# Two of the four weight sums of layer 0's feed-forward units made by accumulating DMAs

## The chip, the cores and the metric

One core of a Trainium2 chip runs the whole program. The metric is the device time of one execution in microseconds, the median over the runs. The engines of a core are TensorE (PE in the profile, with PEld for its weight loads), VectorE (DVE), ScalarE (ACT), GpSimd (POOL) and SyncE (SP). Here SP issues nearly all loads of weights, and POOL issues a few DMAs and small copies.

## The reference

Two layers of a diffusion transformer, in float32, over 512 tokens of x and 256 tokens of context, with a width of 1024 and a hidden width of 2816:

```python
def swiglu(h, w_up, w_down):
    a, b = jnp.split(h @ w_up, 2, axis=-1)
    return (jax.nn.silu(a) * b) @ w_down

def layer(x, ctx, mod_x, mod_c, cos, sin, g1, g2, w_in, ...):
    hx = rmsnorm(x, g1) * (1 + sc1) + sh1
    ...
```

Each layer has a normalisation that is modulated by six vectors (from the matrix w_mod), three groups of heads, an output projection, and then swiglu on the normalised tokens with a residual. In layer 0 swiglu runs on all 768 tokens, in layer 1 on the 512 of x. The change concerns `h @ w_up` in layer 0.

## The kernel before, in words

Float32 products are made of three matmuls each: a tile is split into a rounded part hi (a cast on ACT, line 177) and the rest lo (a subtraction on DVE, line 188), and hi*hi, hi*lo and lo*hi are summed on PE (line 139).

The hidden width of 2816 is cut into 22 columns of 128, f = 0 to 21. For f from 2 on, a *unit* uf makes both halves of its column, the gate and the up half, with seven products where eight quarters would be multiplied plainly. The weights of a unit are two tiles of 128 x 1024, a (the gate half, quarters a11 and a12) and b (the up half, quarters a21 and a22), the quarters being halves of the width of 1024. Four of the seven products need sums of quarters: s1 = a21 + a22 in a tile of its own, e; then a21 + a11 in place, which is s3; s2 = s3 + a22, written over a11; s4 = s2 + a12, over a12. The products run in the order p1 (on a11), p5 (s1), p4 of the unit before (its a22), p6 (s2), p2 (a12), p3 (s4), p7 (s3); the parts are made in the order a11, s1, s2, a12, s4, s3, a22. Each part is cast, its rest is subtracted, and 12 matmuls use it: 128 x 384 each in layer 0, 128 x 256 in layer 1.

The weights come by SP into a ring of four raw slots of 512 KB (line 522), in the order of a plan. A slot is used again when its last reader has been issued. In layer 0 the modulation weights of w_mod go through the same ring, one or two tiles after each unit's a and b; DVE reduces them with line 199 (t<-raw,cst,t). The units are grouped in blocks of columns, by column f in layer 0: (0, 5), (5, 10), (10, 14), (14, 18), (18, 22). Columns 0 and 1 are done plainly. After each block its part of w_down follows. To keep names short, units are numbered u1 to u20 in their order here and in what follows, so u1 to u3 are in the first block, u4 to u8 in the second, u9 to u12, u13 to u16 and u17 to u20 in the others.

An item of the plan may have `sums` set (line 487). Then `w_load`, which issues the loads of an item as soon as a slot is free, takes a tile e for s1 and issues three DMAs on POOL's queue: e <- a21 (line 535), e += a22 (line 536), and in the raw tile, a21 += a11 (line 537). All three read the weights in HBM again, 256 KB each. The part s1 is then cast from e, and the additions of s1 and of a21 + a11 aren't made on DVE. Line 538 tells the planner that such an item is there 4 us later than its loads. In the kernel before only layer 1 does so.

The program is written out unit by unit, and a scheduler places the instructions of each engine, up to a certain point by hand, behind it by the instructions' dependencies and order in the text. Each engine then runs its own row of instructions in order, and stops at one that must wait.

Of the kernel before, what the change touches and what calls it, by code (L numbers as in the profile page):

```python
# [319 lines left out]
def hybrid_kernel(ctx: ExitStack, tc: tile.TileContext, x, c, cx, c_ctx, w_mod, b_mod, norm1_g, norm2_g,  # L320
# [28 lines left out]
    plan = []  # L349

    def cols(src, n):
        return lambda raw: [(raw[:, :n, :], src.rearrange("(k p) n -> p k n", p=P))]

    def w_item(key, n, load, width=P, hold=False, quarters=False):
        plan.append(dict(key=key, n=n, load=load, width=width, hold=hold, mod=False, early=False, read=False, late=False,
                         apart=False, quarters=quarters, sums=None))
# [7 lines left out]
    def mod_items(n):  # L364
        for _ in range(min(n, len(mod_todo))):
            l, g, *at_ = mod_todo.pop(0)
            if len(at_) == 2:
                half, kk = at_
                n0 = g * 512 + half * 256
                src, n_, width = w_mod[l, kk * 512:(kk + 1) * 512, n0:n0 + 256], 4, 256  # L370
            else:
                q, = at_
                src, n_, width = w_mod[l, q * 256:(q + 1) * 256, g * 512:(g + 1) * 512], 2, 512
            plan.append(dict(key=("mod", l, g, *at_), n=n_, load=cols(src, n_), width=width, hold=False, mod=True,
                             early=False, read=False, quarters=False))
# [8 lines left out]
    def in_item(l, name, col):  # L384
        if name == "lr":
            w_item((l, name), 8, lambda raw: [(raw[:, :, j * 32:(j + 1) * 32],
                                               w_in[l, :, col:col + 32].rearrange("(k p) n -> p k n", p=P))
                                              for j in range(3)], 96)
        else:
            w_item((l, name), 8, cols(w_in[l, :, col:col + P], 8))  # L390

    def q_item(l, g):
        def load(raw):
            r = []
            for kv in range(2):
                c0 = W_Q + (kv * 4 + g) * 64
                r.append((raw[:, :, kv * 64:(kv + 1) * 64],
                          w_in[l, :, c0:c0 + 64].rearrange("(k p) n -> p k n", p=P)))
            return r
        w_item((l, "q", g), 8, load)  # L400

    def out1_item(l, j):
        def load(raw):
            ms = slice(j * 256, (j + 1) * 256)
            return [(raw[:, 0:2, :], w_out[l, 0:256, ms].rearrange("(k p) n -> p k n", p=P)),
                    (raw[:, 2:4, :], w_out[l, 768:1024, ms].rearrange("(k p) n -> p k n", p=P))]
        w_item((l, "o1", j), 4, load, 256)

    def up_item(l, q):

        def load(raw):
            ks = slice(q * 2 * P, (q + 1) * 2 * P)
            return [(raw[:, :, j * 2 * P:(j + 1) * 2 * P],
                     w_up[l, ks, j * FF:j * FF + 2 * P].rearrange("(k p) n -> p k n", p=P)) for j in range(2)]
        w_item((l, "up", q), 2, load, 4 * P)
        plan[-1]["late"] = q > 0

    def out2_item(l, m, hold):
        def load(raw):
            ms = slice(m * P, (m + 1) * P)  # L420
            return [(raw[kv * 64:(kv + 1) * 64, 0:4, :],
                     w_out[l, 256 + kv * 256:512 + kv * 256, ms].rearrange("(k p) n -> p k n", p=64))
                    for kv in range(2)]
        w_item((l, "o2", m), 4, load, P, hold)
# [11 lines left out]
    def first_item(l, q):  # L436

        def load(raw):
            ks = slice(q * 2 * P, (q + 1) * 2 * P)
            r = []  # L440
            for i, name in enumerate(FIRST):
                for j in range(3 if name == "lr" else 1):
                    n, c0 = (32, IN_COL[name]) if name == "lr" else (P, IN_COL[name])
                    r.append((raw[:, :, i * P + j * n:i * P + (j + 1) * n],
                              w_in[l, ks, c0:c0 + n].rearrange("(k p) n -> p k n", p=P)))
            return r
        w_item((l, "first", q), 2, load, 3 * P + 96)
        plan[-1]["late"] = q > 0 or l == 0
        plan[-1]["apart"] = q + l == 0
# [9 lines left out]
    for l in range(DEPTH):  # L459
        for q in range(4 if l else 0):  # L460
            first_item(l, q)
        for i, name in enumerate(IN_ORDER):
            if name in FIRST:
                continue
            if name[0] == "q":
                q_item(l, int(name[1]))
            else:
                in_item(l, name, IN_COL[name])
            if l == 0 and i >= 4:
                mod_items(1)  # L470
        for j in range(4):
            out1_item(l, j)
            if l == 0:
                mod_items(2)
        for m in range(NK):
            out2_item(l, m, m >= N_OUT2)
            if l == 0 and m == 0:
                mod_items(1)
        blocks = F_BLOCKS[l]
        for bi, (f0, f1) in enumerate(blocks):  # L480
            for q in range(0 if bi else 4):
                up_item(l, q)
            for f in range(max(f0, 2), f1):
                for half, nm in ((0, "a"), (1, "b")):
                    c0 = half * FF + f * P
                    w_item((l, nm, f), 8, cols(w_up[l, :, c0:c0 + P], 8), quarters=True)
                    plan[-1]["sums"] = (l, f) if l and half else None
                if l == 0:
                    mod_items(2 if f < 14 else 1)
            for m in range(NK):  # L490
                hold = bi == len(blocks) - 1 and m >= N_DOWN
                w_item((l, "d", bi, m), f1 - f0,
                       cols(w_down[l, f0 * P:f1 * P, m * P:(m + 1) * P], f1 - f0), P, hold)
                plan[-1]["late"] = m == 1

                if l == 0 and bi < len(blocks) - 1:
                    mod_items(((0, 1, 1, 2, 1, 1, 1, 0), (0, 1, 0, 1, 0, 1, 1, 0))[bi > 1][m])
# [1570 lines left out]
```

## Time and profile before

| | |
|---|---|
| median of 3 runs | 1621.19 us (1620.47 to 1623.0) |
| profiled execution | 1616.48 us, span 1614.4 us, granted clock 0.998 |
| PE busy | 1574.5 us, 98% of the span |
| DVE, ACT, POOL busy | 1220.2, 755.2, 103.3 us |
| HBM read | 175.08 MB |
| feed-forward units of layer 0 | about 440 to 920 us of the span |
| feed-forward units of layer 1 | about 1240 to 1580 us of the span |

The profile is of one execution. A row of the groups has the line of the code, the engine, what is written and read, the count, the busy time and the mean time of one; then the idle time of the engine before these instructions and what ended most of it. A row of the timeline begins with the start and the length in us.

### The profile page before, as it was taken

Reading aid. Unit: us, or ns where it says so; the run is one execution under the profiler, and the core shown is the slowest. Engines: PE = TensorE matmul, PEld = TensorE weight load, DVE = VectorE, ACT = ScalarE, POOL = GpSimd, SP = SyncE. Lnnn points to the kernel's source line nnn. Section 1 sums busy time; section 2 is a strip of 40 time slices with the busy share of each in tenths; the row PEclk is TensorE's granted clock in tenths of the full one; section 3 lists DMA queues with packets and bytes.
Section 4 is the critical chain, followed back from the end, with each engine's and each line's share of the span. In section 5 each row is a group of like instructions: output and inputs, shape, how many; then the busy total and the mean of one; then the engine's idle time right before and its main releaser. Section 6 shows DMA issues by size and latency. Waiting matters only on the chain.

```text
span 1614.4 us, 29190 instructions
## 1 busy us (share of the span) xinstructions
PE 1574.5 (98%) x11562; PEld 1390.8 (86%) x11562; DVE 1220.2 (76%) x2426; ACT 755.2 (47%) x1588; POOL 103.3 (6%) x118
## 2 busy tenths in 40 slices
PE   7999999999999999999999999998999999999998
PEld 6878677888898899998999988786879999989898
DVE  5687877668886788688888776879787966757576
ACT  4445544453653243242433445464474744636354
POOL 2000000000000000000000000000001112213012
PEclk9999999999999999999999999999999999999999
DMA  9831312154224544435334342211124466848652
GB/s 267 253 96 26 93 53 79 55 169 124 60 79 147 154 141 138 141 123 151 95 109 130 94 123 66 54 38 42 66 76 122 89 148 150 173 121 160 150 123 92
DMA packets 277449, 184.32 MB, mean 114 GB/s; under 512 B 30788, under 2 KB 258624, under 8 KB 277312
## 3 DMA queue, kind: packets, MB, share of 16 engines
q1 hardware_dynamic: 251008, 155.93, 33.7%
q0 software_dynamic: 24480, 21.21, 7.7%
q10 hardware_dynamic: 1824, 5.31, 0.8%
q8 instruction: 91, 1.49, 0.4%
q14 instruction: 46, 0.38, 0.1%
HBM read 175.08 MB, written 7.34 MB: 113 GB/s over the span
## 4 chain that ended last, share of the span: by engine, by line
PE 72%; DVE 11%; DMA 5%; ACT 3%; issue 2%; DVEq 0%; SPq 0%; ACTq 0%
PE main L139 45%; PE bank L139 23%; DMA raw<-in_w_mod_dram 3%; DVE act L188 3%; PE bank L143 3%; DVE wlo L188 1%; DVE t L188 1%; DMA raw<-in_w_up_dram 1%; ACT t L155 1%; DVE t L199 1%; DVE t L216 1%; DVE act L199 1%; DVE mx L207 1%; ACT t L177 1%; ACT act L155 1%
## 5 line engine op out<-in xcount | busy, mean ns | idle before, releaser
L139 PE MATMUL main<-act,whi 128*128 128x512 f32 (+2 forms) x2772 | 667.3, 345 | 5.3 <-DVE act L199 2.5
L139 PEld LDWEIGHTS main<-act,whi 128*128 128x128 f32 x2772 | 460.4, 189 | 62.8 <-issue 12.0
L139 PE MATMUL main<-act,wlo 128*128 128x512 f32 (+2 forms) x1866 | 477.6, 333 | 2.3 <-DVE wlo L188 2.2
L139 PEld LDWEIGHTS main<-act,wlo 128*128 128x128 f32 x1866 | 314.8, 189 | 31.1 <-DVE wlo L188 4.2
L177 ACT CAST whi<-raw 128x512 fp32r<-128x512 f32 (+4 forms) x242 | 181.5, 751 | 292.4 <-PE main L139 200.9
L139 PE MATMUL bank<-act,whi 128*128 128x256 f32 (+4 forms) x1140 | 213.2, 309 | 1.7 <-DVE whi L188 1.0
L139 PEld LDWEIGHTS bank<-act,whi 128*128 128x128 f32 (+1 forms) x1140 | 177.5, 188 | 10.0 <-DVE whi L188 1.6
L139 PE MATMUL bank<-act,wlo 128*128 128x256 f32 (+4 forms) x930 | 182.0, 309 | 0.6 <-DVE wlo L188 0.6
L199 DVE SCALAR_TENSOR_TENSOR act<-main,mods,act 128x256 f32<-128x256 f32 (+1 forms) x162 | 99.3, 616 | 75.7 <-PE main L139 74.0
L139 PEld LDWEIGHTS bank<-act,wlo 128*128 128x128 f32 (+1 forms) x930 | 147.6, 189 | 5.5 <-DVE wlo L188 1.4
L188 DVE TENSOR_TENSOR wlo<-raw,whi 128x1024 fp32r<-128x1024 f32 (+4 forms) x122 | 122.7, 1006 | 22.3 <-ACT whi L177 21.5
L188 DVE TENSOR_TENSOR wlo<-raw,wlo 128x512 fp32r<-128x512 f32 x120 | 81.7, 687 | 39.5 <-ACT wlo L177 38.8
L199 DVE SCALAR_TENSOR_TENSOR t<-raw,cst,t 128x512 f32<-128x512 f32 x126 | 92.3, 747 | 21.3 <-DMA raw<-in_w_mod_dram 20.6
L188 DVE TENSOR_TENSOR whi<-raw,whi 128x512 fp32r<-128x512 f32 x120 | 81.4, 687 | 25.2 <-ACT whi L177 24.0
L155 ACT ACTIVATE t<-bank,nm 128x256 f32<-128x256 f32 (+1 forms) x144 | 69.8, 497 | 60.6 <-DVE nm L199 55.9
L177 ACT CAST wlo<-raw 128x512 fp32r<-128x512 f32 x120 | 74.6, 622 | 42.6 <-PE main L139 17.5
L177 ACT COPY t<-bank 128x512 f32<-128x512 f32 (+3 forms) x131 | 57.3, 452 | 71.8 <-PE bank L139 43.2
L139 PE MATMUL main<-act 128*128 128x256 f32 (+1 forms) x516 | 79.5, 308 | 0.0
L188 DVE TENSOR_TENSOR act<-t,act 128x512 fp32r<-128x512 f32 (+7 forms) x110 | 73.2, 682 | 7.0 <-ACT act L177 5.2
L155 ACT ACTIVATE t<-t 128x256 f32<-128x256 f32 (+3 forms) x108 | 58.1, 538 | 43.2 <-DVE t L188 42.5
L139 PE MATMUL main<-t,whi 128*128 128x512 f32 (+1 forms) x302 | 75.9, 338 | 0.0
L139 PEld LDWEIGHTS main<-act 128*128 128x128 f32 x516 | 70.9, 191 | 5.2 <-ACT t L155 0.4
(161 smaller groups left out, 2005.3 us busy)
## 6 DMA issues: line engine op xcount, KB each, us to landing
raw<-in_w_mod_dram SPq DMA_DIRECT2D x92, 512.0 KB, 4.2
raw<-in_w_up_dram SPq DMA_DIRECT2D x80, 512.0 KB, 4.0
raw<-in_w_in_dram SPq DMA_DIRECT2D x26, 512.0 KB, 3.9
t<-in_w_up_dram POOLq DMA_DIRECT2D x40, 256.0 KB, 5.5
raw<-in_w_down_dram SPq DMA_DIRECT2D x24, 384.0 KB, 4.0
raw<-in_w_down_dram SPq DMA_DIRECT2D x32, 256.0 KB, 2.9
raw<-in_w_down_dram SPq DMA_DIRECT2D x16, 320.0 KB, 3.4
raw<-in_w_up_dram POOLq DMA_DIRECT2D x20, 256.0 KB, 4.7
```

The lines of the kernel that those rows point to most:

```text
L139: self.pin("pe", self.nc.tensor.matmul(out, lhsT, rhs, start=start, stop=stop, **kw))
L143: self.pin("pe", self.nc.tensor.transpose(out, in_, ident))
L155: ins = self.pin("act", self.nc.scalar.activation(out, in_, func, **kw))
L177: self.pin("act", self.nc.scalar.copy(out, in_))
L188: self.pin(eng, self._v(eng).tensor_tensor(out, a, b, op))
L199: self.pin(eng, self._v(eng).scalar_tensor_tensor(out, a, s, b, op0, op1))
L207: self.pin("dve", self.nc.vector.tensor_reduce(out, in_, AX.X, op))
L216: self.pin("dve", self.nc.vector.copy_predicated(out, mask, data))
```

## The change

One condition is dropped, so that the items of layer 0 carry `sums` as well:

```diff
                     w_item((l, nm, f), 8, cols(w_up[l, :, c0:c0 + P], 8), quarters=True)
-                    plan[-1]["sums"] = (l, f) if l and half else None
+                    plan[-1]["sums"] = (l, f) if half else None
```

In the 20 units of layer 0, the 40 DVE additions that make s1 and a21 + a11 go, and 60 DMAs on POOL come in, 40 of them accumulating. Layer 1's own instructions stay as they are, as does the order of SP's loads.

On POOL, where layer 0's units had no row, the second block (u4 to u8) now stands as follows. L535 and L536 make e of a unit (t is the e tile), L537 adds into its raw b.

```order
36 L535 DMA t_6038<-in_w_up_dram 128x4x128
37 L536 DMA t_6038<-in_w_up_dram 128x4x128
38 L537 DMA raw<-in_w_up_dram 128x4x128 x2
39 L535 DMA t_6199<-in_w_up_dram 128x4x128
40 L536 DMA t_6199<-in_w_up_dram 128x4x128
41 L535 DMA t_6342<-in_w_up_dram 128x4x128
42 L537 DMA raw<-in_w_up_dram 128x4x128
43 L536 DMA t_6342<-in_w_up_dram 128x4x128
44 L535 DMA t_6483<-in_w_up_dram 128x4x128
45 L536 DMA t_6483<-in_w_up_dram 128x4x128
46 L537 DMA raw<-in_w_up_dram 128x4x128 x2
47 L535 DMA t_6630<-in_w_up_dram 128x4x128
```

The tiles t_6038, t_6199, t_6342, t_6483 and t_6630 are e of u4 to u8. Row 38 holds the L537 of u4 and of u5, row 46 that of u7 and of u8. So e of u5 (rows 39, 40) and of u8 (row 47 and the one after it) stand behind the L537 of their own unit, u6 has its L535 ahead of it and its L536 behind, and u4 and u7 have both ahead. Of the pairs x2 there are five in layer 0, at u5, u8, u10, u14 and u18; u11, u15, u16, u19 and u20 stand as u6. In layer 1 POOL's rows, which the change leaves alone, begin so:

```order
32 L537 DMA raw<-in_w_up_dram 128x4x128
33 L535 DMA t_13319<-in_w_up_dram 128x4x128
34 L535 DMA t_13460<-in_w_up_dram 128x4x128
35 L536 DMA t_13319<-in_w_up_dram 128x4x128
36 L536 DMA t_13460<-in_w_up_dram 128x4x128
37 L537 DMA raw<-in_w_up_dram 128x4x128
38 L535 DMA t_13602<-in_w_up_dram 128x4x128
39 L536 DMA t_13602<-in_w_up_dram 128x4x128
40 L537 DMA raw<-in_w_up_dram 128x4x128
```

Here the pair of a unit stands ahead of its own L537 (t_13460 is that of the unit whose L537 is row 37).

On DVE, in u8 before, with the waits in brackets: line 188's t_6663<-raw is s1, raw<-raw in row 927 is a21 + a11, and in row 929 s2; row 928 is the rest of s1.

```order
924 L188 TENSOR_TENSOR whi<-raw,whi 128x512 [waits DMAHW3_49,Activation_49]
925 L188 TENSOR_TENSOR t_6663<-raw 128x512 [waits DMAHW4_49]
926 L188 TENSOR_TENSOR t_6555<-bank,t_6555 128x384 [waits PE_49]
927 L188 TENSOR_TENSOR raw<-raw 128x512 [waits DVE_49]
928 L188 TENSOR_TENSOR wlo<-t_6663,wlo 128x512 [waits Activation_49]
929 L188 TENSOR_TENSOR raw<-raw 128x512 [waits DVE_49]
```

And in the changed kernel, where t_6630 is e:

```order
910 L188 TENSOR_TENSOR whi<-raw,whi 128x512 [waits DMAHW3_49,Activation_49]
911 L188 TENSOR_TENSOR raw<-raw 128x512 [waits DMAHW4_49,DMASW6_49,DVE_49]
912 L199 SCALAR_TENSOR_TENSOR t_6505<-raw,cst,t_6505 128x512 [waits DMAHW5_49]
913 L188 TENSOR_TENSOR t_6562<-bank,t_6562 128x384 [waits PE_49]
914 L188 TENSOR_TENSOR mods_137<-bank,bmod 128x4 [waits PE_49]
915 L199 SCALAR_TENSOR_TENSOR t_6505<-raw,cst,t_6505 128x512 [waits DVE_49]
916 L188 TENSOR_TENSOR t_6577<-main,t_6577 128x384 [waits PE_49]
917 L188 TENSOR_TENSOR wlo<-t_6630,wlo 128x512 [waits DMASW0_49,Activation_49]
```

The two additions are gone; s2's addition (row 911) now waits for a DMA of POOL (DMASW) and stands ahead of an eviction and of two steps of the modulation work; the rest of s1 (row 917) stands behind these and waits for a cast that waits for another DMA of POOL.

## The prediction

> **What bounds the kernel now.** I read the windows by stage first, then the groups of VectorE (DVE), then the POOL queue in layer 1, where the operations that the change adds already run, and last the timeline of the units that get them. The windows of the two feed-forward stages that matter (length, then busy time of PE, PEld, DVE, ACT, POOL, clock, DMA share, GB/s):
>
> ```profile
> core 0: us, PE busy (x) PEld busy (x) DVE busy (x) ACT busy (x) POOL busy (x), PEclk, DMA share, GB/s
> 440.00:920.00 480.00, 473.98 (x2812) 444.91 (x2811) 387.60 (x656) 182.78 (x332) 0.00 (x0) 1.00 0.42 124
> ...
> 1240.00:1580.00 340.00, 338.64 (x2393) 316.40 (x2392) 235.03 (x441) 175.60 (x350) 65.62 (x59) 1.00 0.64 137
> ```
>
> Layer 0's feed-forward part is bound by TensorE: of 480.00 us PE works 473.98, so 6.0 us is all that any relief of another engine can bring there. DVE is busy 387.60 us, 81%, but PE hardly ever waits for it. Layer 1 shows the scheme that layer 0 now gets, at 1.4 us of idle PE in 340, though with matmuls over a narrower tile and without the modulation weights, which in layer 0 go through the same four raw slots and DVE.
>
> **What is removed.** The two groups of DVE in that stage, of which 20 additions each go, and the wait that the modulation work has now:
>
> ```profile
> L188 DVE TENSOR_TENSOR raw<-raw 128x512 f32<-128x512 f32 x60 | 41.2, 686 | 0.7
> ...
> L188 DVE TENSOR_TENSOR t<-raw 128x512 f32<-128x512 f32 x20 | 13.8, 689 | 12.2 <-DMA raw<-in_w_up_dram 12.2
> ```
>
> ```profile
> DVE t L199 <- DMA raw<-in_w_mod_dram: 20.6, 21, 2.4
> ```
>
> 20 x 0.689 + 20 x 0.686 = 27.5 us of DVE. All of it lies beside TensorE: removing it is worth between 0 and the 6.0 us that PE idles. I take 0, because those waits stand where a late cast or an eviction comes last, not one of these sums, and keep 6.0 for the range. DVE waits 20.6 us in 21 pieces for modulation weights, so the slots are in demand: a load is issued when a reader lets a slot go.
>
> **What is added.** Per unit three DMAs of 256 KB on POOL, 60 in all, 15.7 MB over 480 us, or 33 GB/s onto 124. That is 157 GB/s, against 137 GB/s in layer 1 at a share of 0.64, so I take layer 1's durations as they are. The order on POOL decides more than the count. POOL takes its rows one by one and stops at one whose data is not there, as layer 1 shows (line, tile, and in brackets the idle time before the row and what ended it):
>
> ```profile
> 1348.23 1.29 POOL L537 DMA_DIRECT2D raw<-in_w_up_dram  x1 [7.37 <-DVE raw L188]
> 1348.98 1.32 POOL L535 DMA_DIRECT2D t<-in_w_up_dram  x1
> 1355.74 1.27 POOL L536 DMA_DIRECT2D t<-in_w_up_dram  x1 [5.44 <-DMA t<-in_w_up_dram]
> 1360.72 1.27 POOL L537 DMA_DIRECT2D raw<-in_w_up_dram  x1 [3.71 <-DMA raw<-in_w_up_dram]
> 1361.47 1.31 POOL L535 DMA_DIRECT2D t<-in_w_up_dram  x1
> 1366.83 1.27 POOL L536 DMA_DIRECT2D t<-in_w_up_dram  x1 [4.05 <-DMA t<-in_w_up_dram]
> ```
>
> ```profile
> 1355.38 0.37 SPq L522 DMA_DIRECT2D raw<-in_w_up_dram  x1
> ```
>
> ```profile
> L536 POOL DMA_DIRECT2D t<-in_w_up_dram x20: 1264/1276/1692, 1246.3 to 1557.5; - x20
> ...
> DMA to landing us min/median/max: 4.6/5.1/6.7
> ```
>
> The L537 at 1360.72 stood waiting for its raw slot, whose load SP had issued at 1355.38, 5.34 us before. L535 follows L537 by 0.75 us. L536 follows L535 by 6.76 and 5.36 us, mean 6.06, since it adds into what L535 must first have landed. Its own landing takes 5.1.
>
> A rule speaks against these prices. The Trainium skill's DMA: Bandwidth & Descriptors, in Anatomy of one DMA — SWDGE (gpsimd) path, gives a DMA of this queue as 2.0 us plus its bytes at 436 GB/s: 2.6 us for 256 KB, an estimate; by it the sum would lose some 2.5 us on each of the two, and with them the waits worked out below. The trace, with 4.6 at the least, does not agree, and the measurement decides.
>
> Now the order of the changed kernel: in layer 0 five units (u5, u8, u10, u14, u18) have L535 and L536 behind their own L537, which is to say behind the landing of their own raw b. In layer 1 the pair mostly stands ahead of it, and what stands behind an L537 is the pair of the next unit. So the sum s1, which a unit needs as its second product, p5, is made only after b has landed. The price of that chain, from the issue of b's load to the first matmul on s1, needs the load's landing in layer 0 and the cast:
>
> ```profile
> raw<-in_w_up_dram SPq DMA_DIRECT2D x80, 512.0 KB, 4.0
> ```
>
> ```profile
> 611.78 0.62 ACT L177 CAST wlo<-t 128x512 fp32r<-128x512 f32 x1 [0.75 <-DVE t L188]
> ```
>
> From b's issue to L537 lie between 4.0 us, the landing alone, and the 5.34 of layer 1; I take 4.54, the landing with half a microsecond for POOL to go on, an estimate. Then 0.75 to L535, 6.06 to L536, 5.1 to its landing, 0.62 for the cast: 17.07 us. The five issues of b and the five starts of p5 before (p5 goes into a "bank" tile, the product ahead of it into "main"; the last row of each fence is u20, used further on):
>
> ```profile
> 554.88 0.37 SPq L522 DMA_DIRECT2D raw<-in_w_up_dram  x1
> 602.72 0.37 SPq L522 DMA_DIRECT2D raw<-in_w_up_dram  x1
> 673.22 0.37 SPq L522 DMA_DIRECT2D raw<-in_w_up_dram  x1
> 769.52 0.37 SPq L522 DMA_DIRECT2D raw<-in_w_up_dram  x1
> 862.62 0.37 SPq L522 DMA_DIRECT2D raw<-in_w_up_dram  x1
> 893.23 0.37 SPq L522 DMA_DIRECT2D raw<-in_w_up_dram  x1
> ```
>
> ```profile
> 570.95 0.51 PE L139 MATMUL bank<-act,whi 128*128 128x384 f32 x2
> 615.51 1.20 PE L139 MATMUL bank<-act,wlo 128*128 128x384 f32 x6
> 689.56 0.68 PE L139 MATMUL bank<-act,wlo 128*128 128x384 f32 x3
> 784.36 0.51 PE L139 MATMUL bank<-act,wlo 128*128 128x384 f32 x2
> 876.87 0.51 PE L139 MATMUL bank<-act,wlo 128*128 128x384 f32 x2
> 905.99 0.33 PE L139 MATMUL bank<-act,wlo 128*128 128x384 f32 x1
> ```
>
> Issue plus 17.07 against p5: u5 571.95 against 570.95, 1.0 late; u8 619.79 against 615.51, 4.3; u10 690.29 against 689.56, 0.7; u14 786.59 against 784.36, 2.2; u18 879.69 against 876.87, 2.8. Together 11.0 us in which TensorE has nothing to do. This is the first term.
>
> The second term is what comes after. Six units (u6, u11, u15, u16, u19, u20) have only L536 behind their own L537: 4.54 + 0.75 + 5.1 + 0.62 = 11.0 us from b's issue. For u20 that is 904.24 against p5 at 905.99: 1.75 us in hand, and no wait by itself. But DVE and ACT take their work in order, and behind a late s1 stand the other casts, the evictions and the modulation work that frees slots. How closely a load follows that work:
>
> ```profile
> 601.16 1.53 DVE L199 SCALAR_TENSOR_TENSOR t<-raw,cst,t 128x512 f32<-128x512 f32 x2
> ...
> 612.65 0.69 DVE L188 TENSOR_TENSOR wlo<-t,wlo 128x512 fp32r<-128x512 f32 x1
> ```
>
> L199 ended at 602.69, and the b load of u8 was issued at 602.72. And s1's subtraction on DVE ended at 613.34, 2.17 us ahead of its matmul at 615.51. When s1 is late by the chain, DVE loses that lead and TensorE does not, so the next loads come up to 2.17 us later than TensorE does, each time. Between 0 (the 1.75 in hand nearly covers it) and 2.17 us for each of the six units; I take the middle, 1.1, since neither end is nearer, so 6.6 us.
>
> The third term is the other sum, a21 + a11, which L537 makes in place, and on which s2, s3 and s4 rest. Layer 1 shows what that costs for the same 20 DMAs:
>
> ```profile
>   DVE raw L188: 2.9, 6
> ```
>
> DVE waited 2.9 us for L537 in 6 of them. Layer 1 has shorter products, but also earlier loads; I take the 2.9 whole, between 0 and the double. SP's own order does not change, and the waits that its loads gain, on the slots into which POOL added, fall on sums landed long before the slot's last reader: nothing, unless POOL runs late by half a unit.
>
> The sum: 11.0 + 6.6 + 2.9 - 0 = 20.5 us on the profiled execution's 1616.48 us (span 1614.4 and 2.1 around it), 1637.0. The median of the three runs is 1621.19, 4.7 higher; with the same difference the forecast is 1621.2 + 20.5 = 1641.7 us.
>
> **The rivals.**
>
> *The sums are hidden, and the relief of DVE counts.* The place is p5 of u8, u14 and u18. If L535 and L536 take some 2.5 us less each there than in layer 1, the chain is 12 us and none of the five is late (the largest, 4.3 us, is gone), and up to 6.0 us of PE's idle time comes back: with most of it, 5, the time is 1616 us. For it speaks layer 1's 1.4 us of idle PE; against it the order, which layer 1 does not have, and the landing, 4.6 at the least. It decides from the point where the chain is under 12.8 us (615.51 - 602.72). The rule of the skill above would bring it about. Chance 0.09.
>
> *The waits and the relief cancel.* The chain is some 2.5 us shorter than I count, u8 is late by 2 and u18 by 0.3, and PE's waits shrink by as much: within 3 us of 1621. Chance 0.07.
>
> *POOL's DMAs are slower than in layer 1.* There DVE is busy 69% of the time, here 81%, and the modulation loads run as well. Layer 1's own spread has this price:
>
> ```profile
> L535 POOL DMA_DIRECT2D t<-in_w_up_dram x20: 749/1308/1337, 1241.2 to 1552.1; - x20
> ```
>
> The issue takes 0.75 to 1.34 us, and the landing of L536 runs up to 6.7, 1.6 over its median. At that end for both L535 and L536 the five units lose 3.2 us more each, 16, and the six 1.6 each, 9.6: 20.5 + 25.6 is 46, 1667 us. Chance 0.14. The Trainium skill's SBUF — State Buffer, under A bandwidth-pool intuition that's wrong (but worth ruling out), says that a DMA from GpSimd's queue waits for its descriptors while DVE holds the port that both share, and gives 3.1 us where it is 0.62 alone; no row here shows such a jump, beside a DVE that is busy two thirds of the time.
>
> That the change does nothing can be ruled out: the 40 DVE additions of layer 0 are gone from the order and 60 DMAs stand in it.
>
> **How the numbers follow.** My own case, at 0.70, gives 1641.7; its bounds run from 11.0 with the whole relief, +5, to 11.0 + 13.0 + 5.8, +30, so 1626 to 1651. The rivals have 0.09 (1616), 0.07 (1621) and 0.14 (1667). The range reaches up into the last one, to 1664, and to 1625 below, which leaves out the first two and the upper end of the third. A measurement of this kernel tells a change of 0.2%, 3.2 us, from none; so faster 0.09, same 0.07, slower 0.84.
>
> **What would show it.** Right: in the profile after, DVE's and ACT's waits for "DMA t<-in_w_up_dram" around 570, 620, 690, 785 and 880 us, PE waiting behind a cast or subtraction of t at p5 of these units, up to 4 us in u8; the idle PE of that stage up from 6 to some 26 us; layer 1 unchanged. Wrong: PE's idle time in the stage at or under 6 us, or its waits in units other than these, or behind an L537 sum rather than s1, or the added time found in layer 1.

## The result, and the profile after

The change made the kernel slower: 1673.11 us (1670.36 to 1676.17, 4 runs) against 1620.83 (4 runs), a ratio of 1.0319, 95% interval 1.0297 to 1.034. That is 52 us where 20.5 were forecast, and 9 us over the upper end of the range. The profiled execution has a span of 1674.4 us, 60.0 more than that before: it lies 3 us over the median of its runs, and the one before 4 us under.

The two feed-forward stages. The first window begins and ends at nearly the same work as that of before and is 54 us longer; the second is as long as that of before, and lies in layer 1, where the other 6 us were lost:

```profile
core 0: us, PE busy (x) PEld busy (x) DVE busy (x) ACT busy (x) POOL busy (x), PEclk, DMA share, GB/s
440.00:974.00 534.00, 492.82 (x2821) 455.36 (x2821) 367.00 (x618) 181.44 (x333) 61.72 (x55) 0.98 0.56 139
```
```profile
core 0: us, PE busy (x) PEld busy (x) DVE busy (x) ACT busy (x) POOL busy (x), PEclk, DMA share, GB/s
1294.00:1634.00 340.00, 334.81 (x2346) 312.37 (x2344) 231.25 (x433) 172.26 (x346) 65.68 (x59) 0.99 0.63 135
```

In layer 0, TensorE idles 534.00 - 492.82 = 41.2 us where it idled 6.0. That is 35 of the 54. The other 19 are not idle time: PE's busy time is 18.8 us longer for the same matmuls (2821 records of matmuls against 2812), and the granted clock has fallen from 1.00 to 0.98. What PE waited for in that stage (us in total, times, longest):

```profile
PE bank L139 <- ACT wlo L177: 14.9, 7, 6.0
PE bank L139 <- ACT whi L177: 11.7, 5, 3.3
PE main L139 <- DVE t L188: 3.7, 2, 2.3
PE bank L139 <- DVE whi L188: 3.6, 2, 3.2
```

Behind the first two rows are, nearly everywhere, casts of s1 that wait for POOL's DMA, behind the fourth the sum s2, for which DVE waits. DVE's waits in the stage:

```profile
DVE raw L188 <- DMA raw<-in_w_up_dram: 40.3, 11, 6.0
DVE t L199 <- DMA raw<-in_w_mod_dram: 36.0, 23, 4.1
```

The first row was not there before: 40.3 us in which DVE stands at s2's addition until L537 has landed. The wait for modulation weights has grown from 20.6 us. And POOL's DMAs take longer here than they did in layer 1 before (5.5 and 4.7 in the page's own table):

```profile
t<-in_w_up_dram POOLq DMA_DIRECT2D x36, 256.0 KB, 6.0
...
raw<-in_w_up_dram POOLq DMA_DIRECT2D x19, 256.0 KB, 6.1
```

The costliest place is u7 and u8. Five views of them, in order: SP's load of u8's b; POOL; DVE at u7's and u8's sum s2 (with the idle time before and what ended it); ACT's cast of u8's s1; PE.

```profile
618.42 0.37 SPq L522 DMA_DIRECT2D raw<-in_w_up_dram  x1
```
```profile
622.82 1.27 POOL L537 DMA_DIRECT2D raw<-in_w_up_dram  x1 [16.16 <-DVE wlo L188]
623.57 1.31 POOL L535 DMA_DIRECT2D t<-in_w_up_dram  x1
631.99 1.29 POOL L536 DMA_DIRECT2D t<-in_w_up_dram  x1 [7.11 <-DMA t<-in_w_up_dram]
```
```profile
612.33 0.69 DVE L188 TENSOR_TENSOR raw<-raw 128x512 f32<-128x512 f32 x1 [5.85 <-DMA raw<-in_w_up_dram]
612.94 0.74 DVE L199 SCALAR_TENSOR_TENSOR t<-raw,cst,t 128x512 f32<-128x512 f32 x1
```
```profile
631.06 0.69 DVE L188 TENSOR_TENSOR raw<-raw 128x512 f32<-128x512 f32 x1 [5.02 <-DMA raw<-in_w_up_dram]
```
```profile
636.64 0.62 ACT L177 CAST wlo<-t 128x512 fp32r<-128x512 f32 x1 [3.20 <-DMA t<-in_w_up_dram]
```
```profile
614.80 1.70 PE L139 MATMUL bank<-act,whi 128*128 128x384 f32 x7 [3.15 <-DVE whi L188]
```
```profile
637.31 4.30 PE L139 MATMUL bank<-act,wlo 128*128 128x384 f32 x12 [6.04 <-ACT wlo L177]
```

From b's issue at 618.42 to the matmul at 637.31 pass 18.9 us; 17.07 were reckoned, and the order is as it was read: L537, then L535, then L536 after L535's landing. L535 took 8.4 us to let L536 start where layer 1 had 6.1. In u7 DVE waited 5.85 us for the L537 sum, and TensorE 3.15. Behind the waiting addition stands L199, which frees a slot for u8's loads: the next unit starts late as well.

The last row also shows the part of the loss that no wait explains: 12 matmuls take 4.30 us, where 12 of 0.173 us would take 2.1. The clock, in windows of 5 us around the gap that ended at 614.80:

```profile
610.00:615.00 5.00, 1.84 (x11) 1.53 (x10) 2.67 (x5) 0.82 (x2) 0.00 (x0) 1.00 0.18 23
615.00:620.00 5.00, 5.00 (x21) 5.00 (x21) 4.93 (x9) 1.59 (x4) 0.00 (x0) 0.66 0.41 120
620.00:625.00 5.00, 5.00 (x31) 5.00 (x30) 4.60 (x8) 3.27 (x6) 2.06 (x2) 1.00 0.51 137
```

In the second window TensorE is busy throughout, but makes 21 matmuls where the third makes 31. Windows of 20 us over the stage, each with 20 us less its clock, add up to 12.2 us lost in this way; before there was none. Between the same two matmuls near the ends of the stage (2902 records in both traces) the changed kernel takes 52.8 us longer: 35.6 us of idle time, 11.9 of low clock, and 5.3 of other busy time. Some of the last lies at the restarts: behind the waits in u6, u16 and u19, at full clock, the first 12 matmuls take 2.73 us, where 12 in an unbroken row take 2.24.

### The profile page after: what moved, and what is told of

It is laid out like the page before. It is cut to its first block, busy times and chain, and to the rows that moved or that the text cites. A ratio compares the mean times of both kernels' runs of the same rounds, so it can differ in the third digit from the quotient of the medians.

```text
span 1674.4 us, 29330 instructions
## 1 busy us (share of the span) xinstructions
PE 1596.2 (95%) x11562; PEld 1404.2 (84%) x11562; DVE 1199.3 (72%) x2386; ACT 751.8 (45%) x1588; POOL 170.4 (10%) x178
## 4 chain that ended last, share of the span: by engine, by line
PE 58%; DVE 13%; DMA 12%; issue 6%; ACT 3%; POOL 1%; DVEq 0%; POOLq 0%; ACTq 0%; SPq 0%
PE main L139 37%; PE bank L139 19%; DMA t<-in_w_up_dram 5%; DMA raw<-in_w_up_dram 4%; DMA raw<-in_w_mod_dram 4%; DVE act L188 3%; PE bank L143 3%; DVE wlo L188 2%; DVE t L199 2%; DVE t L188 1%; ACT t L155 1%; DVE t L216 1%; DVE whi L188 1%; ACT whi L177 1%; DVE mx L207 1%
## 5 line engine op out<-in xcount | busy, mean ns | idle before, releaser
L139 PE MATMUL bank<-act,whi 128*128 128x256 f32 (+4 forms) x1140 | 218.1, 313 | 15.5 <-ACT whi L177 11.7
L139 PE MATMUL bank<-act,wlo 128*128 128x256 f32 (+4 forms) x930 | 189.4, 317 | 19.7 <-ACT wlo L177 14.9
L139 PEld LDWEIGHTS bank<-act,wlo 128*128 128x128 f32 (+1 forms) x930 | 151.0, 193 | 29.0 <-ACT wlo L177 17.1
L199 DVE SCALAR_TENSOR_TENSOR act<-main,mods,act 128x256 f32<-128x256 f32 (+1 forms) x162 | 98.9, 615 | 79.0 <-PE main L139 77.4
L537 POOL DMA_DIRECT2D raw<-in_w_up_dram x40 | 51.5, 1287 | 690.3 <-DVE wlo L188 191.5
L199 DVE SCALAR_TENSOR_TENSOR t<-raw,cst,t 128x512 f32<-128x512 f32 x126 | 92.4, 745 | 36.4 <-DMA raw<-in_w_mod_dram 36.0
L188 DVE TENSOR_TENSOR wlo<-raw,wlo 128x512 fp32r<-128x512 f32 x120 | 81.8, 687 | 35.5 <-ACT wlo L177 34.0
L188 DVE TENSOR_TENSOR raw<-raw 128x512 f32<-128x512 f32 x80 | 55.0, 688 | 50.4 <-DMA raw<-in_w_up_dram 49.3
```

Of the source, the lines that this page charges most:

```text
L139: self.pin("pe", self.nc.tensor.matmul(out, lhsT, rhs, start=start, stop=stop, **kw))
L188: self.pin(eng, self._v(eng).tensor_tensor(out, a, b, op))
L199: self.pin(eng, self._v(eng).scalar_tensor_tensor(out, a, s, b, op0, op1))
L537: S.pin("pool", nc.gpsimd.dma_start(it["raw"][:, :4, :], quarter(1, 1), accum_op=ALU.add))
```

## The experiments

Two questions were put. Which DMAs cost the waiting, by their order on POOL or by being slow; and what the low clock comes from. Times are compared with the kernel before in the same runs (1619.3 to 1620.7 us), differences in us from the medians. t tiles are the pool of 128x768 tiles from which s1's tile comes.

**Only s1 by DMA.** L537 is left out for layer 0 and DVE adds a21 + a11 again.

```diff
-                S.pin("pool", nc.gpsimd.dma_start(it["raw"][:, :4, :], quarter(1, 1), accum_op=ALU.add))
+                if l:
+                    S.pin("pool", nc.gpsimd.dma_start(it["raw"][:, :4, :], quarter(1, 1), accum_op=ALU.add))
...
-                if not self.ib["sums"]:
+                if not self.l or not self.ib["sums"]:
                     S.tt(R["a21"], R["a11"], R["a21"], ALU.add)
```

> Leaves out the DMA that adds a11 into a21 in layer 0; DVE makes that sum again, so nothing on POOL waits for raw b in layer 0 and s1 is still made by two DMAs per unit. Theory A (s1 is late because its DMAs stand behind the unit's own L537 on POOL): the waits at p5 and the slow clock after them go, 1615 to 1628 us. Theory B (POOL's DMAs are slow beside the bursts of SP's loads, in whatever order they stand): s1 still comes late in some units, 1635 us or more. If layer 0's L537 by itself carries little, the time stays above 1650.

Measured 1627.18 us, ratio 1.0039 (1.002 to 1.0059): +6.4. With nothing on POOL that waits for raw b, the waits at p5 are all but gone (PE waits 1.8 us for casts into a bank tile, where it waited 26.6), as the order theory said. Leaving out L537 alone brings back 46 of the 52 us; the next runs take apart, as far as they can, what its traffic, the queue behind it and its own late sum have in that.

**The traffic alone.** The 60 DMAs go into a tile that nobody reads, and DVE makes the sums.

```diff
+                S.pin("pool", nc.gpsimd.dma_start(it["raw"][:, :4, :] if l else e, quarter(1, 1), accum_op=ALU.add))
...
+            if name == "s1" and not self.l:
+                S.gave(self.ib["sum"])
```

> All 60 DMAs of layer 0 are issued, but into a tile that nobody reads; DVE makes the sums of layer 0 as in the kernel before. It shows what the traffic alone costs. Theory A: nobody waits for POOL, so 1618 to 1626 us. Theory B, if the traffic also slows SP's loads by what the ring cannot take: 1630 us or more, with longer waits of DVE for modulation weights (36.0 us in the changed kernel, 20.6 before).

Measured 1635.93 us, ratio 1.0094 (1.0058 to 1.013): +15. More than the order theory allowed. SP's loads of w_up take 4.8 us where they took 3.9 (the medians in this stage; before first):

```profile
raw<-in_w_up_dram SPq DMA_DIRECT2D x38, 512.0 KB, 3.9
```
```profile
raw<-in_w_up_dram SPq DMA_DIRECT2D x38, 512.0 KB, 4.8
```

DVE waits 28.1 us for modulation weights and 19.5 for raw up (20.6 and 12.2 before), and the stage has four windows of 20 us with a low clock, 10.4 us lost, two of which are here:

```profile
520.00:540.00 20.00, 16.89 (x84) 14.44 (x84) 13.08 (x21) 2.28 (x4) 1.31 (x2) 0.83 0.56 169
580.00:600.00 20.00, 17.19 (x82) 16.45 (x81) 12.26 (x21) 7.06 (x13) 4.60 (x4) 0.83 0.66 152
```

Most of the cost is the low clock, then: between the same two matmuls as above TensorE idles 7.1 us more than before. It can't simply be taken as a part of the 52 us, since the same 60 DMAs went out at other times in the changed kernel, where these loads took 4.0 us.

**s1 in a tile of its own, its DMAs ahead.** They go out with the load of a, so that on POOL each pair stands ahead of its own L537.

```diff
+                    plan[-1]["pre"] = (l, f) if l == 0 and not half else None
...
+                        it["sum"] = wp.tile([P, 512], F32, tag="e", name="e", bufs=1)
...
-ROOM = dict(main=3, bank=5, act=20, t3=14)
+ROOM = dict(main=3, bank=5, act=20, t3=13)
```

> s1 in layer 0 is summed into a tile of its own (one buffer, for which the pool of t tiles has 13 instead of 14), its two DMAs issued with the load of a, so on POOL each unit's pair stands ahead of its own L537. All 60 DMAs stay. Theory A: the 27.6 us of waits at p5 in eleven units go, with most of the slow clock; what is left are the 7.3 us of waits for the sums of L537 and some clock: 1625 to 1640 us. Theory B: the DMAs stay slow and s1 still comes late, 1650 us or more.

Measured 1654.93 us, ratio 1.0206 (1.0174 to 1.0239): +34, where 1625 to 1640 was expected of the order theory and 1650 or more of slow DMAs. Here PE waits for the sums of L537 instead:

```profile
PE bank L139 <- DVE whi L188: 9.3, 5, 3.2
PE bank L139 <- DVE wlo L188: 5.5, 5, 1.4
```

The waits for ACT's casts of s1 are gone (1.2 us are left), so the order was part of it: some 18 us of the 52. The larger part is L537.

**The same without L537**, and **the kernel before with 13 t tiles**, its control.

> s1 in layer 0 by two DMAs into a tile of its own (13 t tiles instead of 14), issued with the load of a; DVE makes a21 + a11 again. No DMA of POOL in layer 0 waits for raw b. Order theory: no wait at p5 or p6, only the traffic of 40 DMAs, 1619 to 1630 us, and not under 1615, since TensorE idles only 6.0 us there in the kernel before. If it is over 1640, the order and L537 are not what cost.

> The kernel before with 13 t tiles instead of 14: the control for the kernels with a tile of their own for s1. 1618 to 1626 us if the buffer does not matter; whatever it loses is to be taken off their times.

Measured 1627.93 us, ratio 1.0047 (1.0029 to 1.0066), and 1622.71 us, ratio 1.0023 (1.0009 to 1.0038). So the tile costs 3, s1 by DMA with everything in its favour another 5, and L537 on top 27: it, and not the pair for s1, carries most of the loss.

**L537 alone.** s1 is made on DVE, from a11 and a22.

```diff
-                S.tt(src, R["a21"], R["a22"], ALU.add)
+                S.tt(src, R["a21" if self.l else "a11"], R["a22"], ALU.add)
```

> In layer 0 only the DMA that adds a11 into a21 stays (20 DMAs); DVE makes s1, but from a11 and a22 instead of a21 and a22, so that it needs no order against that DMA: layer 0's result is not the reference's. Two readings of the slow landing of L537 (6.1 us in layer 0 of the changed kernel and 6.5 with s1's tile apart, against 4.7 in layer 1 before). Neighbour on the queue (L535, issued 0.75 us behind it, moves its 256 KB at the same time): the landing falls to 5 us or less and the sum is late only in u2, u3 and u12, 1623 to 1632 us. SP's loads (raw tiles of 512 KB that start while it runs): the landing stays over 6 us, 1642 to 1656 us.

Measured 1642.91 us, ratio 1.0143 (1.0125 to 1.016): +23, from 20 DMAs. The landing in the stage was 5.7 us, between the two expectations; the time is that of the second. So the neighbour on the queue adds some (6.1 and 6.5 with it), but L537 is slower than in layer 1 (4.7) even without one.

**Half of L537**, 128 KB, half the sum left out.

```diff
-                S.pin("pool", nc.gpsimd.dma_start(it["raw"][:, :4, :], quarter(1, 1), accum_op=ALU.add))
+                S.pin("pool", nc.gpsimd.dma_start(it["raw"][:, :4 if l else 2, :], quarter(1, 1) if l else quarter(1, 1)[:, :2, :], accum_op=ALU.add))
```

> As acc_only (the DMA that adds a11 into a21 alone in layer 0, s1 on DVE from a11 and a22), but the DMA adds only half of a11, 128 KB: what size and traffic do. If the price of L537 is its transfer beside SP's loads, the landing falls from 5.7 us to 4 or less and the time to 1625 to 1632 us; if it is a fixed latency, the landing stays over 5 us and the time near acc_only's 1643 us.

Measured 1628.47 us, ratio 1.0055 (1.0032 to 1.0077): +8.5. POOL's DMAs into raw, first L537 alone, then halved:

```profile
raw<-in_w_up_dram POOLq DMA_DIRECT2D x19, 256.0 KB, 5.7
```
```profile
raw<-in_w_up_dram POOLq DMA_DIRECT2D x19, 128.0 KB, 4.7
```

Half the bytes take 4.7 us, not 4 or less: most of the landing did not shrink with the size. But that one microsecond, with half the traffic, took 14 us off the time: DVE's wait for L537 fell from 31.5 to 16.6 us, and TensorE's added idle time between the same two matmuls from 15.2 to 5.1. Which of the two did it, the earlier landing or the smaller traffic, this run can't tell.

**Five raw slots.** Everything of the change stays; the ring gets a slot more, and the t tiles go from 14 to 12 to make room. **The kernel before with 12 t tiles** is the control.

```diff
-    RAWS = 4
+    RAWS = 5
...
-ROOM = dict(main=3, bank=5, act=20, t3=14)
+ROOM = dict(main=3, bank=5, act=20, t3=12)
```

> The changed kernel with five raw slots instead of four (and 12 t tiles instead of 14, to make room). All 60 DMAs stay, and most pairs for s1 still stand behind an L537. If what costs is that b lands too late for a chain of DMAs to be hidden behind it, a slot more brings the loads some 3 to 4 us earlier against the products: 10 to 25 us less than the changed kernel, after what the t tiles cost (control: the kernel before with 12). If the DMAs are slow by themselves or by their traffic, no gain, 1670 us or more.

> The kernel before with 12 t tiles instead of 14: the control for raws5 and z_own. The layer 0 units of z_own waited no more than those before, and its time was lost ahead of and behind them, so the control should lose most of it: 1638 to 1652 us. Near 1621 would mean that the 80 DMAs of z_own cost its 36 us.

Measured 1646.71 us, ratio 1.0161 (1.0131 to 1.0191), and 1639.3 us, ratio 1.0113 (1.0086 to 1.0138). Against its control the change now costs 7 us instead of 52. The stage in both, the five slots first:

```profile
440.00:940.00 500.00, 490.99 (x2875) 458.63 (x2874) 378.33 (x641) 193.26 (x354) 63.67 (x57) 0.99 0.60 149
```
```profile
440.00:940.00 500.00, 494.57 (x2926) 462.82 (x2925) 404.98 (x692) 199.74 (x360) 0.00 (x0) 1.00 0.41 121
```

TensorE idles 9.0 us with the change and five slots, 5.4 in the control, at 149 GB/s, which is more than the change moved (139); the low clock takes 5.0 us more. POOL's order is not the same as in the changed kernel: from u12 on each pair stands ahead of its own L537. But in u5 to u8, u10 and u11 both DMAs of s1 stand behind it, the order that was reckoned at up to 4.3 us a unit, and in these six TensorE waits 1.2 us altogether. So what costs is that b lands too late for the chain of DMAs behind it, not the chain as such. The slot costs the two t tiles, 19 us, so that nothing is won.

**Both sums in tiles of their own**, with the load of a, 80 DMAs, 12 t tiles.

```diff
+                    it["z"] = wp.tile([P, 512], F32, tag="z", name="z", bufs=2)
...
+                    S.pin("pool", nc.gpsimd.dma_start(z, quarter(2, 1)))
+                    S.pin("pool", nc.gpsimd.dma_start(z, quarter(1, 1), accum_op=ALU.add))
```

> Both sums of layer 0 in tiles of their own (one buffer for s1, two for a21 + a11, 12 t tiles instead of 14), each by a plain DMA and an accumulating one issued with the load of a: 80 DMAs, a third more traffic than in the changed kernel, but none waits for raw b. If what costs is that the in-place sum starts only when b has landed: 1622 to 1640 us, in spite of the traffic. If what costs is the traffic: 1650 us or more.

Measured 1656.3 us, ratio 1.0233 (1.0207 to 1.0259). By itself it spoke for the traffic, but it fell to the control: 17 us over 1639.3, about what the traffic alone cost above, and from 440 to 960 us TensorE idled only 9.6 us.

**Filling the gaps**, twice, to see what the low clock is. Matmuls that nobody reads are put ahead of p5 where p5 waited: 12 of them, and then 8 that leave the order of all other instructions as it was.

```diff
+            if self.l == 0 and j == "p5" and self.f - 1 in (5, 6, 8, 10, 11, 14, 15, 16, 18, 19, 20):
+                xh, xl = self.norm.at("b11", 0)
+                for i in range(8):
+                    nc.tensor.matmul(pt, xl[:, :P], xh, start=True, stop=True, skip_group_check=True)
```

> The changed kernel with 12 more matmuls of 128x384 ahead of p5 in the eleven units where p5 waited (u5, u6, u8, u10, u11, u14, u15, u16, u18, u19, u20), into p5's own accumulator, which p5 then starts anew: 11 x 12 x 0.173 = 22.8 us of work, of which some 20.6 fit into the 27.6 us in which TensorE waited there. Theory C (18.8 us of the loss are matmuls at a lower clock, because TensorE idled): the gaps shrink under what lowers the clock and most of the 18.8 us go, 1656 to 1665 us. Without C (the slow matmuls have another cause): 1673 to 1678 us.

> The changed kernel with 8 more matmuls ahead of p5 in the eleven units where p5 waited, with every other instruction of every engine in the changed kernel's own order (with 12 of them POOL's order had changed, so that run told nothing of the clock). 11 x 8 x 0.173 = 15.2 us of work, 1.38 us a unit, where the gaps were 1.4 to 6.0 us, so all of it fits into waiting time. If part of the loss is a lowered clock after a gap: the gaps are 1.4 us shorter each and some of the slow stretches do not come, 1655 to 1668 us. If the gaps do not matter for the speed of the matmuls: 1671 to 1676 us, as the changed kernel.

Measured 1695.02 us, ratio 1.045 (1.0415 to 1.0486), and 1680.75 us, ratio 1.0366 (1.0339 to 1.0394). Both missed. (The 27.6 us of waits in the first text count 2.3 us in u10, which were at the product behind p5.) In the first, POOL's order had changed: u6, u11, u15 and u19 had both DMAs of s1 behind their own L537, and u6's gap was 5.69 us where it was 1.50. That is a further sign of what the order costs, but not a test of the clock. In the second, u5's gap shrank by what was filled (2.89 to 1.52 us), but u6 and u8 waited longer, 2.21 and 7.06 us behind the filling. Idle time in the stage went from 41.2 to 34.1 us, not to 26, and the clock's loss from 12.2 to 10.4, less together than the 15.2 us of added work; so the time rose. Why the waits moved is left open.

**Gaps without DMAs.** In the kernel before, one matmul ahead of p5 in the same eleven units waits for copies on POOL; a is two of 128x384 in a row, b one of 128x128.

```diff
+                nc.gpsimd.tensor_copy(z0[:, :384], self.ta[:, :384])
+                nc.gpsimd.tensor_copy(z[:, :384], z0[:, :384])
...
+                g = nc.tensor.matmul(pt, z[:, :P], xh, start=True, stop=True, skip_group_check=True)
```

> The kernel before, with one matmul of 128x384 ahead of p5 in u5, u6, u8, u10, u11, u14, u15, u16, u18, u19 and u20 that waits for two copies in a row on POOL of p1's evicted product; nothing reads what it makes. TensorE's order is otherwise that of the kernel before, no DMA is added. It makes eleven gaps on TensorE with no change of the traffic, an estimated 2.5 to 4 us each, 28 to 44 us. If the lowered clock comes from gaps alone: stretches of a granted clock near a half stand behind most of them, and the time rises by 8 to 20 us more than the gaps add up to. If the slow matmuls of the changed kernel came from its DMAs: the clock stays at 1.00 and the time rises by the gaps and nothing else.

> As stall_a with one short copy (128x128) in place of two of 128x384, so that the eleven gaps are shorter, an estimated 1 to 1.5 us, 11 to 17 us together. If the clock answers to the length of a gap: no stretch of a low clock, and the time rises by the gaps alone, to 1631 to 1638 us. If any gap lowers it: 8 us more or over.

Measured 1652.95 us, ratio 1.0195 (1.0166 to 1.0225), and 1635.27 us, ratio 1.01 (1.0078 to 1.0123). The waits that were made, a and b:

```profile
PE bank L1177 <- POOL t L1174: 23.4, 11, 2.6
```
```profile
PE bank L1176 <- POOL t L1173: 12.7, 11, 1.4
```

a cost 33.7 us for 23.4 us of waits and 1.9 of added matmuls, 8.4 more; b 16.0 for 12.7 and 1.9, 1.4 more. The clock behind the gap of 2.2 us in u5 of a (ended at 578.47), and behind that of 1.3 us in b (at 572.82):

```profile
580.00:585.00 5.00, 5.00 (x21) 5.00 (x21) 2.98 (x5) 1.30 (x3) 0.00 (x0) 0.67 0.24 71
585.00:590.00 5.00, 5.00 (x31) 5.00 (x30) 4.17 (x7) 3.68 (x7) 0.00 (x0) 1.00 0.38 107
```
```profile
575.00:580.00 5.00, 5.00 (x31) 5.00 (x30) 2.82 (x5) 2.04 (x4) 0.00 (x0) 1.00 0.31 91
```

Without any DMA added, a has five windows of 20 us with a low clock in the stage, 8.8 us lost; b, where the made gaps are 1.4 us at the most, has none. Four of the five lie behind the eleven made gaps (1.8 to 2.6 us), not behind most of them as expected; the fifth lies behind a wait of 1.9 us for DVE that the kernel before has as well (2.0 us, there without a low clock). So the low clock comes from gaps without any DMA, but not from each gap of 2 us.

The trace's records of the granted clock show which. In each trace the low stretches begin whole multiples of 3.413 us apart, and each lasts 3.413 us or a multiple of it (but for the last, at the end of the span). So the clock is granted by fixed windows of that length, and what goes with a fall is how much of one window TensorE was busy. From 440 to 1010 us of the 16 traces, 30 windows at full clock were busy for less than 44%, and the next window was low behind each; of 12 with 44 to 50%, behind 8; of 2579 with more, behind 2. In the changed kernel the gaps of 2.16 us (u14) and 1.65 us (u18) left 35% and 49% of one window, and the clock fell; those of 2.44 us (u15) and 2.36 us (u19) were divided over two windows, of which the emptier kept 54% and 53%, and it did not fall.

## Why the prediction was wrong, step by step

Two steps failed: layer 1's durations and waits were taken over for layer 0, worst for the in-place sum of L537 (2.9 us reckoned, some 8 us of direct waits and a late queue behind it), and the sum had no term for a low clock (12 us). The waits found below are 12.7 + 12.5 + 8 + 2.3 = 35.5 us, which is the added idle time of the stage; 20.5 us were reckoned.

**Sign, place and order: right.** TensorE bounds the stage, the relief of DVE brings nothing that can be seen (DVE's busy time on the page fell from 1220.2 to 1199.3 us while TensorE's idle time rose), POOL stops in order at a DMA whose data is not there, and s1 is late in u5, u8, u14 and u18.

**The first term, 11.0 us for s1 behind its own L537: nearly right in all, in part by luck.** PE's gaps at p5 were 2.89 (u5), 6.04 (u8), 2.16 (u14) and 1.65 us (u18), 12.7 together; u10, reckoned at 0.7, did not wait. One by one they were reckoned at 1.0, 4.3, 2.2 and 2.8: the chain was dearer than its price (18.9 us against 17.07 in u8), and u10 and u18 made up for part of it.

**The second, 6.6 us for the six units after: too small.** 1.50 (u6), 3.34 (u11), 2.44 (u15), 1.40 (u16), 2.36 (u19) and 1.48 (u20), 12.5 together. L535 and L536 were taken from layer 1 at 5.1; in layer 0 they took 6.0.

**The third, 2.9 us for the sums of L537: the step that failed most.** Its direct waits came out 5 us over their price, as those of the second term did by 6, but L537 costs more than these waits. It was read from DVE's waits in layer 1, at 4.7 us of landing and with b's load early. In layer 0 the four slots are shared with the modulation weights, b lands shortly before it is needed, and L537 takes 6.1: DVE waited 40.3 us for it, and PE some 8 us directly (3.15 in u7, 3.9 in u2 and u3, 1.0 in u12), besides what it shifted; another 2.3 us in u10 came of a late load of modulation weights. How short the slack was could have been read: in the kernel before, s2's addition began 2.3 to 11.8 us after b's landing, 6.6 in the median of the 14 units whose landing the trace records, and a DMA of 5 to 6 us had to fit in. L537 alone costs 23 us (1642.91), and 27 with s1's pair out of the way (1654.93 against 1627.93). "I take layer 1's durations as they are" was wrong in size, and the wrong thing to compare: half of L537's bytes, with a microsecond less of landing, was worth 14 us, and with a slot more the change cost 7 us instead of 52.

**The clock: not in the sum at all.** Of the 54 us in layer 0, 35 are idle time and 12.2 a low granted clock behind gaps; the rest, 5 to 6 us, is busy time that no low clock explains. stall_b has 3 us of such time in its profiled execution (its units take 16.6 us longer for 11.6 more idle time and 1.9 of matmuls). Slow restarts are a part of it; whether they are all stays open. The forecast took a wait at its length. The Trainium skill's TensorE: Matmul & The Clock Gate, in Part 1: The HAM clock gate (the "warmup" mystery), says that TensorE's clock is halved after an idle window of some 3.4 us. The trace agrees in the half (21 matmuls in 5 us, 0.66 in the mean) and shows windows of 3.41 us, but the window need not be idle: gaps of 1.65, 2.16 and 2.18 us brought the low clock, each mostly within one window, while gaps of 2.36 and 2.44 us, divided over two, did not.

**Layer 1 unchanged: wrong by 6 us.** One wait of 3.8 us for an L537 sum stands there at 1553.59 that was not there before, with a stretch of low clock behind it. Its own instructions are the same; why that L537 landed later is left open.

**The rival.** The time came out nearest to "POOL's DMAs are slower than in layer 1" (1667, chance 0.14), and they were, 6.0 to 6.1 us. But the longer issue to landing was only part of it; without the clock its sum would have been too high for the idle time (46 against 35), so that it came near by luck in part. Whether DVE's work slowed GpSimd's DMAs, the rule named beside that rival, no run here tested; half the bytes or a neighbour less moved the landing between 4.7 and 6.5 us.

## What to carry to other kernels

A DMA that adds into a tile in place starts only when that tile has landed, and so is paid on the path wherever loads are not a whole DMA latency early; a scheme that is hidden in one stage says nothing of another with the same code and fewer free slots. Reckon the slack from landing to use first, and the queue's order second: here 5 to 6 us of latency met some 6.6 us of slack, and a microsecond (with half of that DMA's traffic) was worth 14 us in all. Where TensorE is the bound, price a new gap at its length, and at 1.7 us of slow matmuls more (half of 3.41) where it takes over half of one window of the clock: here four of eleven gaps of 1.8 to 2.6 us did, and none of those up to 1.4 us.

## What the runs showed of the hardware that was not expected

- Gaps on TensorE cost more than their length where they bring a low clock: 33.7 us for 23.4 us of waits and 1.9 of work (stall_a), against 16.0 for 12.7 and 1.9 where they don't (stall_b). The low clock holds for 3.41 us or a multiple, at half the rate (21 matmuls of 128x384 in 5 us, then 31).
- Whether the clock falls is not set by the length of the gap alone, but by how busy TensorE was in one fixed window of 3.41 us: under 44% it fell each time (30 of 30 from 440 to 1010 us of the 16 traces), over 50% hardly ever (2 of 2579). In the changed kernel it fell behind gaps of 1.65 and 2.16 us and not behind 2.36 and 2.44.
- An accumulating DMA of 128 KB landed in 4.7 us, of 256 KB in 5.7, in the same place; with a second DMA behind it on the queue in 6.1 to 6.5.
- 60 DMAs of 256 KB that nobody waits for cost 15 us; beside them loads of 512 KB landed in 4.8 us instead of 3.9, TensorE idled 7.1 us more, and 10.4 us went to the low clock.
